# Gaps of 32 to 64 bytes between SBUF tiles, so that weight slabs and the tiles multiplied with them lie 64 bytes apart by the remainder of 128

## The chip, the core and the metric

The kernel runs on one core of one Trainium2 chip. The metric is the device time of one execution in microseconds (us). Each kernel is timed in several runs and the median is quoted; one execution of it was also recorded by the hardware profiler, and everything read from rows below is of that one execution.

## What is computed

The input is one sequence of 256 tokens with 1024 features, all in float32. It goes through two blocks.

```python
# first block, one layer
h = rms_norm(x, norm_mix)
proj = h @ w_in                       # q, k, v of three branches, gates, pool input, merge gates
a = nsa_attention(...) @ w_branch_attn
b = pool_mixer(u_pool, ...) @ w_branch_pool
x = x + (ga * a + gb * b) @ w_out
x = x + square(relu(rms_norm(x, norm_mlp) @ w_ff1)) @ w_ff2      # 4096 wide
# second block, two layers: attention in the first, a gated convolution in the second
x = x + sliding_window_attention(...)        # or short_gated_conv(...)
x = x + peer_ffn(rmsnorm(x), w_query, sub_keys, expert_u, expert_v)
# peer_ffn: for each token 8 heads pick 16 of 16384 experts by two top-16 lists of 128 keys;
# y = sum over picked e of  g_e * gelu(x . u_e) * v_e
```

The two `peer_ffn` layers are the bulk: each reads two tables (`peer_u`, `peer_v`) of 16384 x 1024 floats, and the kernel multiplies with all 16384 experts, with weights that are zero for experts that a token did not pick.

## The kernel before

**Weights as a stream.** All weight matrices are cut into slabs of 128 x 1024 floats (4096 bytes in each partition), in the order in which they are used (`plan`). The class `Stream` loads a slab into one of three buffers `wraw` (a DMA queued on SyncE), and splits it: ScalarE rounds it into `wh` (line 70), VectorE, or GpSimd for some slabs of the expert stages, writes the remainder into `wl` (line 71). `wh` and `wl` have four buffers each, and the split runs up to three slabs ahead of the slab in use, so a slab's buffers become free when TensorE is done with the slab four before it.

**Three matmuls for one.** The activations are split likewise: a tile such as `xh` holds a rounded part `xh[:, 0]` and the rest `xh[:, 1]`. Each product is three matmuls in the type fp32r: `wh` with `xh[:, 0]`, `wh` with `xh[:, 1]`, `wl` with `xh[:, 0]` (the function `dense3`). In these dense stages the weight slab is the stationary operand (128 columns, loaded into the array ahead of its matmul, rows PEld of the profile) and the activation tile is the moving operand, 256 columns (the tokens). All matmuls are issued from one helper, `mm`, line 174; the profile tells them apart by their tiles: `mm<-xh,wh` writes the PSUM tile `mm` from `xh` and `wh`.

**The stages**, in the order of the run, with the tile that is multiplied with the slabs: input projections (`xh`), the compression of keys and values (`movh`, stationary, 30 columns), pool and merge parts (`ph`, `mh`), attention output (`oh`), `w_out` and `w_ff1` (`xh`), `w_ff2` (`mid`, four tiles), the second attention (`xh`, then `xo`), and for each expert layer the query (`xh`), the 128 slabs of `peer_u` (`xh`), and the 128 slabs of `peer_v`. Between the two expert layers the convolution multiplies with `xh` and with `zh`, a tile on the place of `gA0` that the profile calls `gA`. In the `peer_v` stage (the function `mix`) the roles are turned: the activations `h` (the buffer `xh0`) are stationary, 128 columns, and the slab is the moving operand, 512 columns; the profile calls it `g<-wh,xh` and `g<-wl,xh`.

**Side work in the `peer_u` stages.** While TensorE works through the 128 slabs, VectorE does first the top-16 search (`topk`, lines 1075 to 1147), and then, in 32 groups of eight tokens, builds one-hot tables (`onehot`, lines 1175 to 1179, float16), which 16 small float16 matmuls a group turn into gate weights (`spread`; the profile calls them `g<-misc` and `g<-lows,misc`), and multiplies the results by them (line 1197). Each engine's order is the program's order here (`manual_schedule`), and the amount of side work issued with each slab is a fixed budget.

**Where tiles lie.** A pool's tiles lie one behind the other in SBUF in the order of the calls, each rounded up to 32 bytes in a partition; a tile is never moved. `x` starts at byte 4224, a multiple of 128. Behind it `cols` takes 352 bytes, and all that follows in the pool `glob` and in `xhp` has a size that is a multiple of 128, so `wraw`, `wh`, `wl`, `misc`, `row`, `xh0` and `xh1` all start at a remainder of 96 when their address is divided by 128. The built program's addresses give:

| tile | role beside the slabs `wh`, `wl` (remainder 96) | remainder before | distance before | remainder after | distance after |
|---|---|---|---|---|---|
| `xh0`, `xh1` (also `h` of `mix`) | moving; stationary in `mix` | 96 | 0 | 32 | 64 |
| `movh` | stationary, 30 columns | 32 | 64 | 32 | 64 |
| `ph`, `mh`, `oh` | moving | 0 | 32 | 32 | 64 |
| `mid` (four) | moving | 32 | 64 | 32 | 64 |
| `xo` (two) | moving | 96 | 0 | 32 | 64 |
| `zh` (place of `gA0`) | moving | 96 | 0 | 32 | 64 |

All rows and columns of these tiles that a matmul starts at lie at multiples of 128 bytes from the tile's start (but for `movh`), so the distance holds for every matmul of a row of the table. `x` stays at 0; `row`, `misc` and `wraw` stay at 96; `iota2`, `lows`, `gA1` go from 96 to 32.

Of the kernel before, what the change touches and what calls it, by code (L numbers as in the profile page):

```python
# [8 lines left out]
F32 = mybir.dt.float32  # L9
# [9 lines left out]
P = 128  # L19
# [87 lines left out]
def build(tc, a):  # L107
# [172 lines left out]
    xhp = ctx.enter_context(tc.tile_pool(name="xhp", bufs=1))  # L280

    def xh_tile(i):
        return xhp.tile([P, 2, KD, T], F32R, name=f"xh{i}")

    def sq_tile():
        return glob.tile([P, KD, T], F32, name="misc")
# [19 lines left out]
    bp = b1.enter_context(tc.tile_pool(name="b1", bufs=1))  # L306
    pa = b1.enter_context(tc.tile_pool(name="pa", bufs=1, space=PSUM))

    xh = xh_tile(0)
    sq = sq_tile()  # L310
    for i in range(0, KD, 2):
# [16 lines left out]
    kvc = bp.tile([P, 2, T], F32, name="kvc", tag="t2")  # L328
    kc2 = bp.tile([P, 2, 2, T], F32, name="kc2", tag="t4")
    mov = bp.tile([P, 2, 16, 2, 15], F32, name="mov")  # L330
    movh = bp.tile([P, 2, 2, 16, 30], F32R, name="movh")
    qr = bp.tile([P, 3, 2, T], F32, name="qr")
    qk = bp.tile([P, 3, 2, T], F32, name="qk")
# [98 lines left out]
        PE.transpose(ps[:, 0, t * 24:(t + 1) * 24], gT[:, t * P:(t + 1) * P], ident[:24, :24])  # L432
    S.activation(gates.rearrange("p t g -> p (t g)"), ps[:, 0, :48], AF.Tanh, scale=0.5)

    oh = bp.tile([P, 2, 4, T], F32R, name="oh")

    def attention():
# [268 lines left out]
    ff = ExitStack()  # L706
    fpool = ff.enter_context(tc.tile_pool(name="ff", bufs=1))
    pf = ff.enter_context(tc.tile_pool(name="pf", bufs=1, space=PSUM))
    mid = [fpool.tile([P, 2, KD, T], F32R, name=f"mid{i}") for i in range(4)]
    rel = [fpool.tile([P, 2, T], F32, name=f"rel{i}") for i in range(2)]  # L710
    sq2 = fpool.tile([P, 2, T], F32, name="sq2")
# [786 lines left out]
```

## Time and profile before

| | |
|---|---|
| median of 3 runs | 2226.88 us (2226.35 to 2228.36) |
| the profiled execution: its own time | 2228.21 us |
| its span in the trace | 2226.4 us |
| mean granted TensorE clock | 0.996 of full speed |
| TensorE busy (PE, weight loads apart) | 98% of the span |
| VectorE (DVE), ScalarE (ACT), GpSimd (POOL) busy | 72%, 49%, 7% |
| bytes moved by DMA | 382.67 MB, mean 172 GB/s |

The busy time of TensorE is that of overlapping matmuls whose ends are modelled: one matmul stands in the trace for some 280 ns, but the next starts long before that. How fast TensorE goes is therefore read from the starts of matmuls that follow each other, and this text calls the time from one start to the next the pitch.

### The profile page before, as it was taken

What the parts mean: (1) busy time and instruction counts of PE and PEld (TensorE: products, weight loads), DVE (VectorE), ACT (ScalarE), POOL (GpSimd) and SP (SyncE); (2) the same over time, 40 slices, a digit from 0 to 9 for tenths busy, and PEclk for the clock granted to TensorE, in tenths of its full rate; (3) what the DMA queues carried; (4) which work ended last, traced back from release to release, by engine and by line L of the source; (5) the groups of instructions that cost most, each with busy time, mean ns of one, the idle gap of its engine ahead of it and who ended that gap; (6) DMA issues with size and microseconds to landing.
All of it is one profiled execution on the core that took longest, in us unless ns stands there. A gap on an engine that the chain in (4) does not pass through costs nothing.

```text
span 2226.4 us, 39574 instructions
## 1 busy us (share of the span) xinstructions
PE 2186.1 (98%) x15892; PEld 2040.8 (92%) x15892; DVE 1594.8 (72%) x2802; ACT 1084.5 (49%) x1707; POOL 148.2 (7%) x66
## 2 busy tenths in 40 slices
PE   8999999999989999999999999999899999999999
PEld 7899999999989999988888889999899999888887
DVE  7757656666998899755555566779988986555555
ACT  5555555564434444445454454544444435454454
POOL 0000000001442000000000000044300000000000
PEclk9999999999999999999999999999999999999999
DMA  6435555334544444455555555545444445555554
GB/s 208 152 133 180 181 190 190 105 134 151 189 143 167 152 161 157 164 196 190 197 190 196 191 172 180 191 164 174 154 150 162 152 147 195 197 191 196 191 190 150
DMA packets 105625, 382.67 MB, mean 172 GB/s; under 512 B 11985, under 2 KB 12385, under 8 KB 105185
## 3 DMA queue, kind: packets, MB, share of 16 engines
q1 hardware_dynamic: 105120, 378.04, 48.9%
q8 instruction: 124, 2.03, 0.4%
q0 software_dynamic: 320, 2.11, 0.3%
q14 instruction: 61, 0.49, 0.1%
HBM read 379.05 MB, written 1.05 MB: 171 GB/s over the span
## 4 chain that ended last, share of the span: by engine, by line
PE 84%; DVE 10%; issue 3%; ACT 2%; DMA 1%; SPq 0%; ACTq 0%; DVEq 0%
PE mm L174 46%; PE g L174 34%; DVE wl L71 3%; PE s L174 2%; DVE gA L1117 2%; ACT wh L70 1%; PE o L174 1%; DVE gA L1115 1%; DVE gA L1114 1%; DMA wraw<-in_w_in 0%; DVE gA L1197 0%; DVE lows L1178 0%; DVE misc L1179 0%; DMA x<-in_x 0%; DVE gA L1087 0%
## 5 line engine op out<-in xcount | busy, mean ns | idle before, releaser
L71 DVE TENSOR_TENSOR wl<-wraw,wh 128x1024 fp32r<-128x1024 f32 (+1 forms) x660 | 824.0, 1249 | 512.5 <-ACT wh L70 509.1
L174 PE MATMUL mm<-xh,wh 128*128 128x256 f32 x6240 | 1148.6, 286 | 9.1 <-ACT wh L70 6.9
L70 ACT CAST wh<-wraw 128x1024 fp32r<-128x1024 f32 (+1 forms) x716 | 747.0, 1054 | 726.3 <-PE g L174 332.6
L174 PEld LDWEIGHTS mm<-xh,wh 128*128 128x128 f32 x6240 | 979.9, 193 | 11.7 <-ACT wh L70 7.5
L174 PE MATMUL mm<-xh,wl 128*128 128x256 f32 x3120 | 889.1, 285 | 13.2 <-DVE wl L71 13.2
L174 PE MATMUL g<-wh,xh 128*128 128x512 f32 x2048 | 632.6, 389 | 0.0
L174 PEld LDWEIGHTS mm<-xh,wl 128*128 128x128 f32 x3120 | 602.4, 193 | 15.5 <-DVE wl L71 15.4
L174 PEld LDWEIGHTS g<-wh,xh 128*128 128x128 f32 x2048 | 384.4, 188 | 79.8
L174 PE MATMUL g<-wl,xh 128*128 128x512 f32 x1024 | 398.4, 389 | 0.0
L174 PEld LDWEIGHTS g<-wl,xh 128*128 128x128 f32 x1024 | 192.2, 188 | 39.5
L71 POOL TENSOR_TENSOR wl<-wraw,wh 128x1024 fp32r<-128x1024 f32 x56 | 142.7, 2547 | 285.2 <-ACT wh L70 271.5
L1199 ACT ACTIVATE gA<-g 128x96 f32<-128x96 f32 (+14 forms) x72 | 23.4, 343 | 243.8 <-DVE gA L1197 225.2
L1218 DVE TENSOR_TENSOR xh<-gA,xh 128x256 fp32r<-128x256 f32 x224 | 93.5, 418 | 0.0
L1217 ACT CAST xh<-gA 128x256 fp32r<-128x256 f32 x224 | 90.1, 403 | 0.0
L174 PE MATMUL mm<-mid,wh 128*128 128x256 f32 x512 | 87.1, 276 | 0.0
L1234 ACT ACTIVATE gA<-mm 128x512 f32<-128x512 f32 (+15 forms) x112 | 55.6, 496 | 63.4 <-PE mm L174 63.4
L174 PEld LDWEIGHTS mm<-mid,wh 128*128 128x128 f32 x512 | 77.0, 188 | 0.0
L174 PE MATMUL g<-misc 128*128 128x128 f16 x512 | 67.0, 221 | 9.9 <-DVE misc L1179 9.9
L174 PEld LDWEIGHTS <-misc 128*128 128x128 f16 x1024 | 59.8, 98 | 13.1 <-issue 6.8
L174 PE MATMUL mm<-mid,wl 128*128 128x256 f32 x256 | 70.7, 276 | 0.0
L174 PE MATMUL g<-lows,misc 128*128 128x128 f16 x512 | 66.4, 220 | 0.0
L1197 DVE SCALAR_TENSOR_TENSOR gA<-g,gA 128x512 f32<-128x512 f32 (+30 forms) x114 | 57.1, 538 | 0.0
(346 smaller groups left out, 1570.2 us busy)
## 6 DMA issues: line engine op xcount, KB each, us to landing
wraw<-in_peer_u SPq DMA_DIRECT2D x256, 512.0 KB, 3.5
wraw<-in_peer_v SPq DMA_DIRECT2D x256, 512.0 KB, 3.5
wraw<-in_w_ff SPq DMA_DIRECT2D x64, 512.0 KB, 4.4
wraw<-in_w_query SPq DMA_DIRECT2D x32, 512.0 KB, 3.6
wraw<-in_w_in SPq DMA_DIRECT2D x29, 512.0 KB, 4.0
wraw<-in_w_cin SPq DMA_DIRECT2D x24, 512.0 KB, 3.6
wraw<-in_w_qkv SPq DMA_DIRECT2D x12, 512.0 KB, 4.1
wraw<-in_w SPq DMA_DIRECT2D x8, 512.0 KB, 3.5
```

The costliest lines, as they stand in the source:

```text
L70: nc.scalar.copy(h[:, s], r[:, s])
L71: (nc.gpsimd if j in self.pooled else nc.vector).tensor_sub(l[:, s], r[:, s], h[:, s].bitcast(F32))
L174: PE.matmul(out, l, r, start=start, stop=stop, skip_group_check=True)
L1114: V.tensor_tensor(eq, pb, J[:, None].to_broadcast([P, 2, NCAND, 16]), op=OP.is_equal)
L1115: V.tensor_tensor(prod, eq, code[:, hq:hq + 2, :, None].to_broadcast([P, 2, NCAND, 16]), op=OP.mult)
L1117: V.reduce_sum(sel[:, hq:hq + 2], prod.rearrange("p h c k -> p h k c"), axis=AX.X)
L1197: V.scalar_tensor_tensor(v, pr[:, i0:j], 2.0 ** -15, v, op0=OP.mult, op1=OP.mult)
L1199: S.activation(d[:, j - i0:i1 - i0, t0:t0 + 8], pr[:, j:i1], AF.Copy, scale=2.0 ** -15)
L1217: S.copy(w[0], gA(e))
L1218: V.tensor_sub(w[1], gA(e), w[0].bitcast(F32))
L1234: S.activation(d[:, :, n:], ps[:, :, n:], AF.Gelu)
```

## The change

Four small tiles that nothing reads or writes are allocated, and so push what is allocated behind them. `gap` (64 bytes) moves both `xh` and every pool opened later by 64 bytes; `gap1` moves `movh` and what stands behind it in its pool by 64 more, `gap2` moves `oh` and what follows by 32 more, `gap3` moves `mid` by 64 more. The weight slabs stay where they are. The table above has the remainders. The instructions of all engines, their order and the semaphores that they wait for are the same one by one as before; only addresses differ.

```diff
@@ -306,6 +306,8 @@
     pa = b1.enter_context(tc.tile_pool(name="pa", bufs=1, space=PSUM))
 
+
+    xhp.tile([P, 16], F32, name="gap")
     xh = xh_tile(0)
     sq = sq_tile()
@@ -328,6 +330,7 @@
     mov = bp.tile([P, 2, 16, 2, 15], F32, name="mov")
+    bp.tile([P, 16], F32, name="gap1")
     movh = bp.tile([P, 2, 2, 16, 30], F32R, name="movh")
@@ -432,6 +435,7 @@
 
+    bp.tile([P, 8], F32, name="gap2")
     oh = bp.tile([P, 2, 4, T], F32R, name="oh")
@@ -706,6 +710,7 @@
     pf = ff.enter_context(tc.tile_pool(name="pf", bufs=1, space=PSUM))
+    fpool.tile([P, 16], F32, name="gap3")
     mid = [fpool.tile([P, 2, KD, T], F32R, name=f"mid{i}") for i in range(4)]
```

## Rows read from the trace of the kernel before

**Rows 1.** The page: busy time by engine, and the chain by line

```profile
PE 2186.1 (98%) x15892; PEld 2040.8 (92%) x15892; DVE 1594.8 (72%) x2802; ACT 1084.5 (49%) x1707; POOL 148.2 (7%) x66
...
PE mm L174 46%; PE g L174 34%; DVE wl L71 3%; PE s L174 2%; DVE gA L1117 2%; ACT wh L70 1%; PE o L174 1%; DVE gA L1115 1%; DVE gA L1114 1%; DMA wraw<-in_w_in 0%; DVE gA L1197 0%; DVE lows L1178 0%; DVE misc L1179 0%; DMA x<-in_x 0%; DVE gA L1087 0%
```

**Rows 2.** Matmuls by form: count, busy us, mean ns of one, idle before

```profile
L174 PE MATMUL mm<-xh,wh 128*128 128x256 f32 x6240 | 1148.6, 286 | 9.1 <-ACT wh L70 6.9 <-ACT gA L1234 0.7 <-ACT xh L195 0.6
L174 PE MATMUL mm<-xh,wl 128*128 128x256 f32 x3120 | 889.1, 285 | 13.2 <-DVE wl L71 13.2
L174 PE MATMUL g<-wh,xh 128*128 128x512 f32 x2048 | 632.6, 389 | 0.0
...
L174 PE MATMUL mm<-mid,wh 128*128 128x256 f32 x512 | 87.1, 276 | 0.0
...
L174 PE MATMUL mm<-xo,wh 128*128 128x256 f32 x128 | 25.6, 292 | 0.6 <-ACT xo L915 0.3 <-DVE xo L916 0.2
...
L174 PE MATMUL mm<-wh,xh 128*128 128x256 f32 x64 | 12.9, 298 | 0.0
...
L174 PE MATMUL mm<-mh,wh 128*128 128x256 f32 x64 | 11.4, 279 | 0.0
```

**Rows 3.** Timeline of PE, query stage, first and last of ten groups (start, us)

```profile
504.00 0.40 PE L174 MATMUL mm<-xh,wh 128*128 128x256 f32 x2
...
507.24 0.40 PE L174 MATMUL mm<-xh,wh 128*128 128x256 f32 x2
```

**Rows 4.** Timeline of PE, `w_ff2` stage, first and last of ten groups

```profile
329.83 0.39 PE L174 MATMUL mm<-mid,wh 128*128 128x256 f32 x2
...
332.89 0.28 PE L174 MATMUL mm<-mid,wh 128*128 128x256 f32 x1
```

**Rows 5.** Timeline of PE, stage of `mh`, first and last of eleven groups

```profile
158.22 0.40 PE L174 MATMUL mm<-mh,wh 128*128 128x256 f32 x2
...
161.76 0.40 PE L174 MATMUL mm<-mh,wh 128*128 128x256 f32 x2
```

**Rows 6.** Timeline of PE, `peer_v` stage, first and last of four groups

```profile
1000.48 0.62 PE L174 MATMUL g<-wh,xh 128*128 128x512 f32 x2
...
1002.52 0.62 PE L174 MATMUL g<-wh,xh 128*128 128x512 f32 x2
```

**Rows 7.** Timeline of PE, small float16 matmuls of one group, third and last

```profile
871.59 0.22 PE L174 MATMUL g<-misc 128*128 128x128 f16 x1
...
872.33 0.22 PE L174 MATMUL g<-lows,misc 128*128 128x128 f16 x1
```

**Rows 8.** Weight loads by form: count, busy us, mean ns of one

```profile
L174 PEld LDWEIGHTS mm<-xh,wh 128*128 128x128 f32 x6240 | 979.9, 193 | 11.7 <-ACT wh L70 7.5 <-ACT xh L195 0.9 <-DVE xh L196 0.9
...
L174 PEld LDWEIGHTS g<-wh,xh 128*128 128x128 f32 x2048 | 384.4, 188 | 79.8
...
L174 PEld LDWEIGHTS mm<-mid,wh 128*128 128x128 f32 x512 | 77.0, 188 | 0.0
```

**Rows 9.** Windows in `peer_u`: length, busy PE, PEld, DVE, ACT, POOL, clock, DMA

```profile
580.00:600.00 20.00, 20.00 (x169) 20.00 (x168) 19.67 (x98) 9.28 (x11) 7.85 (x4) 1.00 0.58 193
580.00:704.00 124.00, 115.53 (x944) 114.78 (x943) 120.48 (x285) 54.15 (x63) 52.35 (x20) 0.98 0.48 165
...
1500.00:1624.00 124.00, 115.01 (x939) 114.22 (x938) 120.19 (x262) 52.09 (x61) 50.25 (x20) 0.98 0.46 160
...
860.00:880.00 20.00, 20.00 (x192) 19.87 (x191) 18.77 (x28) 8.59 (x18) 0.00 (x0) 1.00 0.46 159
892.00:917.00 25.00, 23.87 (x230) 23.54 (x226) 20.76 (x29) 8.39 (x18) 0.00 (x0) 1.00 0.41 139
```

**Rows 10.** VectorE by form: count, busy us, mean ns of one

```profile
L1175 DVE TENSOR_TENSOR misc<-iota,row 128x1024 f16<-128x1024 f16 x64 | 43.7, 683 | 0.0
...
L236 DVE TENSOR_TENSOR misc<-misc 128x512 f32<-128x512 f32 x18 | 12.4, 688 | 0.4
...
L689 DVE TENSOR_TENSOR x<-x,sq 128x512 f32<-128x512 f32 x4 | 2.8, 692 | 0.1
```

## The prediction, before the changed kernel was run

> **What bounds the kernel now.** I read the page first, then the matmuls by form, then the starts of single matmuls in each stage, then windows of the stretches where VectorE is fullest. On the page TensorE is busy 98% of the span, and the chain that ended last runs for 80% through two kinds of its matmuls, the dense ones (46%) and those of `peer_v` (34%) [rows 1]. The reader should see that waits are small: the 9360 dense matmuls on `xh` have 22.3 us of idle time before them in all [rows 2]. So in most stages the time is the number of matmuls times their pitch, and the pitch is what this change can touch.
>
> The pitch differs between stages that do the same thing. In the query stage, where slab and `xh` are 0 apart by the remainder, 27 matmuls start in 507.24 - 504.00 = 3.24 us, 120.0 ns each [rows 3]. In the `w_ff2` stage, where slab and `mid` are 64 apart, 27 start in 332.89 - 329.83 = 3.06 us, 113.3 ns each [rows 4]. With `mh`, 32 apart, 30 start in 3.54 us, 118.0 ns [rows 5]. Columns, type and slabs are the same in all three. Weight loads go along: 193 ns in the mean with `xh`, 188 with `mid` [rows 8]. So three distances are ordered as the change supposes, and its own distance, 64, has been run already, by 768 matmuls.
>
> **The change, part by part.** No instruction is added, removed or reordered, so its whole cost or gain is in the durations.
>
> *Dense matmuls at distance 0.* These are 6240 + 3120 on `xh`, 128 on `xo` with `wh` and half as many with `wl`, as many again on `zh`, and 64 + 32 with `xh` stationary [rows 2]: 9360 + 192 + 192 + 96 = 9840. Taken at `mid`'s pitch each is 120.0 - 113.3 = 6.7 ns shorter (3.24 - 3.06 us over 27): 65.6 us. Bounds: nothing, if `mid` is fast for another reason; 65.6 us, since `mid` is the fastest pitch of this size that the trace has.
>
> *Those at distance 32:* 96 on `mh`, as many on `oh` and 12 on `ph`, 4.7 ns each: 1.0 us. *`mid` and `movh`* keep their distance: 0.
>
> *The `peer_v` stage.* 2048 + 1024 matmuls of 512 columns [rows 2] go from 0 to 64 too. Their pitch is 2.04 us over 9, 226.7 ns [rows 6]. That is two times 113.3, and the float16 matmuls of 128 columns start every 0.74 us / 13 = 56.9 ns, half of it [rows 7]: 0.443 to 0.445 ns a column in all three. At distance 0 this stage thus already runs at the pace a column that the dense matmuls reach only at 64, and its weight loads take 188 ns, as with `mid`, not 193 [rows 8]. A longer moving stream seems to leave time to load weights. I take 0. Bounds: a gain of the same 6.7 ns for each weight load, 3072 x 6.7 = 20.5 us; a loss of 6.7 to 13.3 ns (once or twice, by columns, what a bad distance costs at 256), 20.5 to 41 us.
>
> *What VectorE takes back.* While TensorE gets faster, the splits and the side work stay, and where VectorE is full nothing is gained. In the window from 580 to 600 us VectorE is busy 19.67 of 20 us during 169 matmuls, so 19.67 / 169 x 24 = 2.79 us a slab [rows 9]. A slab is 24 matmuls: 2.88 us now, 2.72 after. VectorE becomes the limit from about 580 us on, and stays it until the search ends near 704 us (120.48 of 124 us busy, and TensorE already waits). The end of that stretch is then VectorE's. The gain of its 944 matmuls is lost, 6.3 us, and of the 939 in the second layer, 6.3 us [rows 9]. TensorE's waits for `wl` and the one-hot tables grow by that much.
>
> In the groups that follow, one group is 48 dense and 16 small matmuls. Late in them, from 860 to 880 us, 192 matmuls are three groups: VectorE 18.77 / 3 = 6.26 us a group, TensorE 6.67 now and 6.67 - 48 x 0.0067 = 6.35 after [rows 9]. VectorE would be 98.6% full there, just not the limit; I take off 1 us a layer, my choice between 0 and all. At the groups' end, 892 to 917 us, TensorE waits for VectorE already (23.87 of 25 us): 230 matmuls less 48 small ones lose 1.2 us, and the same in the second layer. For the start and the two attentions, where matmuls alternate with short chains on VectorE and ScalarE, I take off 2 us, without a row of their own. Together: 12.6 + 2.0 + 2.4 + 2.0 = 19.0 us. Bounds: about 10 (slack absorbs half of it), or 37 if VectorE limits all the groups, below.
>
> *Other engines.* Loads must come every 2.72 us a slab instead of 2.88; the new need is 0.524 MB / 2.72 us = 193 GB/s, which the window from 580 to 600 us already moved [rows 9]. ScalarE is about half busy. VectorE and ScalarE operands move by 64 bytes too. Of their cost a row speaks: additions of 128x512 take 688 ns with all operands at remainder 96 (line 236) and 692 with `x` at 0 and `sq` at 32 (line 689) [rows 10]. I take 0; the splits at line 71 don't move at all.
>
> *Sum.* 65.6 + 1.0 - 19.0 = 47.6 us. From the profiled execution's own 2228.2 us (span 2226.4) that gives 2180.6; the median is 1.3 us below that execution, so **2179 us**.
>
> The Trainium skill speaks against the change: "TensorE: Matmul & The Clock Gate", in the section "Step-by-step: what each phase is for", says that TensorE has two independent read ports to SBUF and that loading the next weights doesn't take bandwidth from the running matmul. By that the sum would be 0, and the time 2227 us. The pitches 120.0 and 113.3 do not agree with it, unless something else makes `mid` fast.
>
> **The rivals.**
>
> 1. *`peer_v` gains too.* The cost would hang on each weight load, whatever the moving columns: 20.5 us more, 2159 us. For it: the distance is 0 there as well. Against it: the pace a column, equal to that at distance 64, and the loads of 188 ns.
> 2. *`peer_v` loses.* 0 may be a good distance there and 64 a bad one: 20.5 to 41 us less, 2200 to 2220 us. No row has that stage at another distance, so nothing speaks for it but that.
> 3. *VectorE takes more.* If it limits all groups of each layer, their gain goes too (704 to 892 us is 28 periods of 6.7 us with 48 dense matmuls each: 28 x 48 x 6.7 ns = 9.0 us a layer): 18 us, 2197 us. For it: 98.6% leaves no room for an order of work that waits.
> 4. *The distance that counts is of 256, not 128.* `mid` now lies 64 behind the slabs by 256, `xh` will lie 192. If 192 is as good as `mh`'s 224 only (118.0 ns), the dense matmuls gain 2.0 x 9840 = 19.7 us, `mid`, which moves to 192 too, loses 4.7 x 768 = 3.6, VectorE takes 5.7 (19.0 x 2.0 / 6.7): 10 us, 2217 us.
> 5. *The change doesn't do what it says.* `mid` is fast for a reason other than its place: 2227 us. Against it: `mh` and `oh` lie between, as their distance does. By the skill's rule above this would be the outcome.
> 6. *Slower.* VectorE's one-hot comparisons (lines 1175, 1176) read `iota2` at 32 and `row` at 96 after the change, and line 1178 writes `lows` at 32 from `misc` at 96. If VectorE minds distances, these grow in a stage where it is nearly full. To turn the gain of 47.6 us into a loss over 64 groups takes 0.74 us a group beyond the free 0.09: 0.83 us over three instructions of 0.68, 0.28 us or 41% each. The 4 ns between 688 and 692 [rows 10] are far from that.
>
> **How the numbers follow.** My forecast 0.63 (its own range 2170 to 2190, by the losses of 10 to 28 us); rival 1 0.12; rival 2 0.05; rival 3 0.07; rival 4 0.05; rival 5 0.05; rival 6 0.03. A range from 2155 to 2198 holds nearly all of the first, rival 3, and most of rival 1: about 0.8. A measurement of this kernel tells 0.2% (4.5 us) from no change. Faster by more than that: all but rivals 5 and 6, 0.92; same 0.05; slower 0.03.
>
> **What would show it.** Right: starts of dense matmuls 113.3 ns apart in the query, `w_ff1`, convolution and early `peer_u` stages; their weight loads at 188 ns; `mid` unchanged; `peer_v` at 226.7 ns; VectorE still 19.9 of 20 us busy near 640 us, and TensorE's idle time before `wl` matmuls up from 13.2 us [rows 2] by about 10. Wrong: a pitch other than 113.3 ns (the distance rule fails), `peer_v` at 220 or 233 ns and more, or VectorE's instructions at other durations than before.

## The result, and the profile after

The changed kernel took 2241.5 us (median of 5 runs, 2238.36 to 2244.63), the kernel before 2228.36 us (5 runs, 2226.35 to 2231.41): ratio 1.0058, 95% interval 1.0044 to 1.0073. It is slower by 0.6% where 2.2% faster was forecast.

Every engine's work is what it was, only the pace of TensorE's matmuls differs. The page after (busy time by engine, then the chain by line) answers to [rows 1]: dense matmuls hold less of the chain (`mm`, 36% after 46%), those of `peer_v` about as much, VectorE's splits `wl` more.

```profile
PE 2192.5 (98%) x15892; PEld 2025.7 (90%) x15892; DVE 1595.2 (71%) x2802; ACT 1083.5 (48%) x1707; POOL 149.3 (7%) x66
...
PE mm L174 36%; PE g L174 33%; DVE wl L71 7%; ACT wh L70 3%; DMA wraw<-in_peer_u 2%; PE s L174 2%; DVE gA L1202 2%; DVE lows L1183 1%; PE o L174 1%; DVE gA L1122 1%; ACT act L1236 1%; ACT gA L1239 1%; DVE misc L1180 1%; DVE misc L1181 0%; DVE gA L1119 0%
```

The timeline of TensorE after (start, duration; rows between left out) shows three things. First two rows: a dense stage in its fast stretch, 9 matmuls in 189.13 - 188.11 = 1.02 us, 113.3 ns each. Next two, `w_ff1`: 27 in 3.18 us, 117.8 ns. Next two, `w_ff2` on `mid`: 27 in 3.18 us, 117.8 ns, where it was 113.3 [rows 4]. Last two, `peer_v`: 39 in 9.09 us, 233.1 ns, where it was 226.7 [rows 6].

```profile
188.11 0.39 PE L174 MATMUL mm<-xh,wh 128*128 128x256 f32 x2
...
189.13 0.39 PE L174 MATMUL mm<-xh,wh 128*128 128x256 f32 x2
...
239.83 0.40 PE L174 MATMUL mm<-xh,wh 128*128 128x256 f32 x2
...
243.01 0.40 PE L174 MATMUL mm<-xh,wh 128*128 128x256 f32 x2
...
329.93 0.40 PE L174 MATMUL mm<-mid,wh 128*128 128x256 f32 x2
...
333.11 0.40 PE L174 MATMUL mm<-mid,wh 128*128 128x256 f32 x2
...
1000.21 0.63 PE L174 MATMUL g<-wh,xh 128*128 128x512 f32 x2
...
1009.30 0.63 PE L174 MATMUL g<-wh,xh 128*128 128x512 f32 x2
```

Weight loads after, by form (count, busy us, mean ns of one, idle before), answer to [rows 8]: with `xh` they fell from 193 to 190 ns, not to 188; in `peer_v` they stand at 188 as before, though its pitch grew.

```profile
L174 PEld LDWEIGHTS mm<-xh,wh 128*128 128x128 f32 x6240 | 962.6, 190 | 17.1 <-ACT gA L1239 6.8 <-ACT wh L70 6.8 <-ACT xh L195 0.9
...
L174 PEld LDWEIGHTS g<-wh,xh 128*128 128x128 f32 x2048 | 384.8, 188 | 92.7
...
L174 PEld LDWEIGHTS mm<-mid,wh 128*128 128x128 f32 x512 | 78.2, 187 | 0.0
```

The windows after (columns as in [rows 9]) show VectorE at 19.91 of 20 us in the search, and the end of the groups, 892 to 917 us, with TensorE busy 20.31 us, where it was 23.87: it waits there for ScalarE and VectorE (rows below, with the prediction's step on VectorE). The first row is a stretch of the `qkv` stage in which TensorE was granted 0.50 of its clock, the lower level of 1.2 GHz.

```profile
389.80:396.60 6.80, 6.80 (x34) 6.80 (x33) 2.55 (x7) 1.25 (x2) 0.00 (x0) 0.50 0.46 154
580.00:600.00 20.00, 20.00 (x172) 20.00 (x171) 19.91 (x103) 9.63 (x12) 8.96 (x4) 1.00 0.62 199
...
892.00:917.00 25.00, 20.31 (x198) 19.45 (x197) 20.79 (x29) 8.40 (x18) 0.00 (x0) 1.00 0.39 127
```

The same stretch of the kernel before, in the same view, has the full clock:

```profile
389.80:396.60 6.80, 6.80 (x59) 6.80 (x60) 4.71 (x12) 1.75 (x3) 0.00 (x0) 1.00 0.46 154
```

Stage lengths, worked out as the start of a stage's first matmul to that of the next stage, say where the 13.3 us (spans 2226.4 and 2239.7) come from:

| stage | before | after | difference |
|---|---|---|---|
| `peer_v`, layers 0 and 1 | 349.49 + 354.27 | 359.64 + 364.36 | +20.2 |
| `w_ff2` (on `mid`) | 87.06 | 90.45 | +3.4 |
| `qkv` (with the half clock) | 65.00 | 67.76 | +2.8 |
| all other stages together | | | -13.1 |
| of these, `w_ff1` | 93.19 | 91.36 | -1.8 |
| of these, the searches of both `peer_u` | 166.23 + 165.74 | 163.97 + 164.47 | -3.5 |
| of these, the groups of both `peer_u` | 217.99 + 218.66 | 218.61 + 218.56 | +0.5 |

### The profile page after: what moved, and what is told of

Read it like the earlier page. It is cut to its first block, busy times and chain, and to the rows that moved or that the text cites. A ratio compares the mean times of both kernels' runs of the same rounds, so it can differ in the third digit from the quotient of the medians.

```text
span 2239.7 us, 39574 instructions
## 1 busy us (share of the span) xinstructions
PE 2192.5 (98%) x15892; PEld 2025.7 (90%) x15892; DVE 1595.2 (71%) x2802; ACT 1083.5 (48%) x1707; POOL 149.3 (7%) x66
## 4 chain that ended last, share of the span: by engine, by line
PE 73%; DVE 15%; ACT 5%; issue 3%; DMA 3%; POOL 0%; SPq 0%; ACTq 0%; DVEq 0%
PE mm L174 36%; PE g L174 33%; DVE wl L71 7%; ACT wh L70 3%; DMA wraw<-in_peer_u 2%; PE s L174 2%; DVE gA L1202 2%; DVE lows L1183 1%; PE o L174 1%; DVE gA L1122 1%; ACT act L1236 1%; ACT gA L1239 1%; DVE misc L1180 1%; DVE misc L1181 0%; DVE gA L1119 0%
## 5 line engine op out<-in xcount | busy, mean ns | idle before, releaser
L71 DVE TENSOR_TENSOR wl<-wraw,wh 128x1024 fp32r<-128x1024 f32 (+1 forms) x660 | 825.3, 1251 | 530.8 <-ACT wh L70 529.4
L174 PE MATMUL mm<-xh,wh 128*128 128x256 f32 x6240 | 1130.3, 283 | 13.6 <-ACT wh L70 6.3
L174 PEld LDWEIGHTS mm<-xh,wh 128*128 128x128 f32 x6240 | 962.6, 190 | 17.1 <-ACT gA L1239 6.8
L174 PE MATMUL mm<-xh,wl 128*128 128x256 f32 x3120 | 879.9, 282 | 14.4 <-DVE wl L71 14.4
L174 PE MATMUL g<-wh,xh 128*128 128x512 f32 x2048 | 645.7, 396 | 0.0
L174 PEld LDWEIGHTS mm<-xh,wl 128*128 128x128 f32 x3120 | 591.7, 190 | 17.3 <-DVE wl L71 17.2
L174 PE MATMUL g<-wl,xh 128*128 128x512 f32 x1024 | 404.8, 395 | 0.0
L174 PE MATMUL g<-misc 128*128 128x128 f16 x512 | 67.1, 221 | 10.9 <-DVE misc L1184 10.9
```

Of the source, the lines that this page charges most:

```text
L71: (nc.gpsimd if j in self.pooled else nc.vector).tensor_sub(l[:, s], r[:, s], h[:, s].bitcast(F32))
L174: PE.matmul(out, l, r, start=start, stop=stop, skip_group_check=True)
```

## The experiments

Three theories stood against each other. The first: the remainder of 256 counts, not of 128. The diff brought most tiles to 64 by 128, but by 256 `xh`, `mid` and `peer_v`'s tile came to 192 and only the smaller tiles (`ph`, `mh`, `oh`, `movh`) to 64. The second: places themselves count (which addresses), not distances. The third, on the part that remains: pitch isn't set by the distance alone. Beside them stood two questions of size: does `peer_v` cost the 20 us, and does VectorE take back what the dense matmuls gain? Distances below are slab minus tile by 256; the matmul means are over 764 starts of `w_ff1` (on `xh`), 768 of `w_ff2` (on `mid`) and 1531 of `peer_v` in layer 0, each in the one trace of its kernel.

**The changed kernel again**, to see what one profile repeats.

> The changed kernel, unaltered, profiled a second time. Theory A (at a distance of 64 by 128 a dense matmul can settle at one of two pitches, 113.3 or 117.7 ns, and what happened just before picks which): the same addresses, but the stretches at 113.3 ns need not be the same ones; query0, w_out and xo, each partly at 113.3 ns in the first trace, may come out otherwise, and mid may be at 113.3 again. Theory B (the distance by 256 decides: 64 fast, 192 slow): mid, xh and zh at 117.7 ns in the same places throughout. Both: peer_v at about 233 ns, time about 2241 us.

Measured: 2242.92 us (before 2231.62 beside it); 117.51, 117.78 and 233.33 ns, the means of the first profile to the hundredth. Most of the fast stretches come again too, the 113.3 ns stretch of `w_out` above among them, but not all: in the query stage of layer 1 no matmul settled at 113.3 ns in the first profile and 19% did in the second, in the search of layer 1 none and 7%. So the pitch of a stage is not fixed by the program.

**One gap of another size.** Ahead of `xh` alone, in the kernel before, with n = 8, 32, 40, 48 or 64 for 32, 128, 160, 192 or 256 bytes. Everything allocated behind it moves too:

```diff
+    xhp.tile([P, n], F32, name="gap")
     xh = xh_tile(0)
```

128 bytes:

> The kernel before with one gap of 128 bytes ahead of xh0 instead of the four gaps: xh, xo and zh stay 0 from the slabs by the remainder of 128 (128 by 256), mid stays 64 by 128 but goes from 64 to 192 by 256. Theory A: xh at 120.0 ns and peer_v at 226.7 ns as before; mid at 113.3 or 117.7 ns. Theory B: mid at 117.7 ns, xh anything but 120.0 is possible. Time: A 2227 (2230 if mid is slow), B unlike that if 128 by 256 is a place of its own.

192 bytes:

> The kernel before with one gap of 192 bytes ahead of xh0: xh, xo and zh lie 64 from the slabs by 128, and slab minus tile is 64 by 256 (192 in the changed kernel); mid goes to a distance of 0. Theory A: xh mostly at 117.7 ns with stretches of 113.3, mid at 120.0 ns, peer_v about 233 ns, time about 2243 us. Theory B: xh at 113.3 ns throughout, mid at 120.0; time near 2195 us with peer_v at 233 ns, 2175 us with peer_v at 226.7.

32 bytes:

> The kernel before with one gap of 32 bytes ahead of xh0: xh, xo and zh lie 32 before the slabs' remainder plus 128 (slab minus tile 96 by 128, as mh and oh before), mid 32 apart. Theory A: xh at about 118 ns as mh before, mid at about 118, peer_v between 226.7 and 233 ns. Theory B: xh at 118 ns too (224 by 256 as mh before). The run tells what a distance of 32 does to peer_v, on which neither has a row.

256 bytes:

> The kernel before with one gap of 256 bytes ahead of xh0: all distances by 256 are as before, those by 512 are not. If 256 is the period: xh 120.0 ns, mid 113.3 ns, peer_v 226.7 ns, 2228 us. If the period is longer (or peer_v needs the tiles at another multiple): peer_v 233.3 ns, 2248 us.

160 bytes:

> The kernel before with one gap of 160 bytes ahead of xh0: xh at slab minus tile 96 by 256, mid at 160, peer_v's operands 160 apart. Theory A for peer_v: 233.3 ns, as at each other distance but 0. For dense no forecast beyond the ones seen, between 113.3 and 120.0 ns: the run fills in two distances.

Measured, with the kernel before, the changed one and the next experiment (distance: mean pitch):

| kernel | `w_ff1` | `w_ff2` | `peer_v` | time, us |
|---|---|---|---|---|
| before | 0: 119.98 | 64: 113.36 | 0: 226.71 | 2228.36 |
| after | 192: 117.51 | 192: 117.78 | 192: 233.33 | 2241.5 |
| 128 bytes | 128: 118.66 | 192: 117.78 | 128: 233.33 | 2250.52 |
| 192 bytes | 64: 113.56 | 128: 118.67 | 64: 233.32 | 2227.94 |
| 32 bytes | 224: 116.67 | 32: 118.33 | 224: 233.33 | 2238.35 |
| 160 bytes | 96: 117.33 | 160: 119.99 | 96: 233.33 | 2246.80 |
| 256 bytes | 0: 119.97 | 64: 113.36 | 0: 226.71 | 2226.45 |
| all moved by 64 | 0: 119.99 | 64: 113.36 | 0: 226.71 | 2230.08 |

(Times of the gaps are of one run each, beside kernels before at 2226 to 2232 us.) The row that tells 128 from 256 is that of 128 bytes, which leaves `xh` at 0 by 128: by theory A `xh` stays at 120.0 and `peer_v` at 226.7 ns. They came to 118.7 and 233.3, `peer_v` with 9 matmuls in 2.10 us:

```profile
999.86 0.63 PE L174 MATMUL g<-wh,xh 128*128 128x512 f32 x2
...
1001.96 0.63 PE L174 MATMUL g<-wh,xh 128*128 128x512 f32 x2
```

The changed kernel and the one with 192 bytes both have `xh` at 64 by 128, at 192 and 64 by 256. With 192 bytes the timeline of `w_ff1` has 27 matmuls in 3.06 us, 113.3 ns; the next two rows, `peer_v` of the same kernel, have 9 in 2.10 us, 233.3 ns; the last two, late in `peer_v` of layer 1, 9 in 2.06 us, 228.9 ns:

```profile
239.93 0.39 PE L174 MATMUL mm<-xh,wh 128*128 128x256 f32 x2
...
242.99 0.39 PE L174 MATMUL mm<-xh,wh 128*128 128x256 f32 x2
...
1000.21 0.63 PE L174 MATMUL g<-wh,xh 128*128 128x512 f32 x2
...
1002.31 0.40 PE L174 MATMUL g<-wh,xh 128*128 128x512 f32 x1
...
2198.39 0.62 PE L174 MATMUL g<-wh,xh 128*128 128x512 f32 x2
...
2200.45 0.62 PE L174 MATMUL g<-wh,xh 128*128 128x512 f32 x2
```

So in these two large stages 64 by 256 gives the fast pitch for 256 columns and 192 the slow one. For 512 columns, the five distances other than 0 give 233.3 ns, but for the last 324 of 3072 matmuls at 64. That one gap of 192 bytes ends level with before (2227.94): the dense gain and `peer_v`'s loss cancel.

The small stages do not keep to this. In the changed kernel `mh` and `oh` lie at 64 by 256, yet all their matmuls ran at 117.8 ns, and with the gap of 32 bytes they lie at 192 and ran at 113.3. In the rows, `mh` in the changed kernel has 27 matmuls in 3.18 us, 117.8 ns:

```profile
154.85 0.40 PE L174 MATMUL mm<-mh,wh 128*128 128x256 f32 x2
...
158.03 0.40 PE L174 MATMUL mm<-mh,wh 128*128 128x256 f32 x2
```

In the kernel called best below `mh` lies at 64 too, and has 27 in 3.06 us, 113.3 ns:

```profile
155.73 0.39 PE L174 MATMUL mm<-mh,wh 128*128 128x256 f32 x2
...
158.79 0.39 PE L174 MATMUL mm<-mh,wh 128*128 128x256 f32 x2
```

Both distances thus have the same two pitches, 113.3 and 117.8 ns.

**Distances or places.** The gap stands ahead of everything, slabs included, so that all places move by 64 and no distance does.

```diff
+    glob.tile([P, 16], F32, name="gap")
     x = glob.tile(...)
```

> The kernel before with a gap of 64 bytes ahead of x, the first tile: every tile moves by 64 bytes and no distance changes. Theory A (distances): all pitches as before, 120.0, 113.3 and 226.7 ns, 2228 us. Rival C (a tile's own remainder counts): xh at 32 by 128 would run as in the changed kernel, 117.7 ns, and peer_v at 233.3 ns, 2241 us.

Measured: 2230.08 us, and all three pitches are those of before (last row of the table). Distances count, places don't, as far as one move by 64 bytes shows; with 256 bytes doing nothing either, the period of 256 fits.

**`peer_v` back at 0, the rest as changed.** The stationary weights `h` of `mix` get a tile of their own at distance 0:

```diff
+        hv = []
...
-            w = h[:, 0, e % 4], h[:, 1, e % 4]
+            if not hv:
+                hv.append(glob.tile([P, 2, 4, T], F32R, name="misc"))
+            w = hv[0][:, 0, e % 4], hv[0][:, 1, e % 4]
...
-            wh, wl = (h[:, p, e % 4, t * P:(t + 1) * P] for p in range(2))
+            wh, wl = (hv[0][:, p, e % 4, t * P:(t + 1) * P] for p in range(2))
...
-            res.extend((xh_tile(1), sq_tile()))
+            res.append(xh_tile(1))
...
+            res.append(sq_tile())
```

> The changed kernel, but the stationary operand of the peer_v stage lies in the buffer misc, at remainder 96 like the slabs, instead of in xh0. Theory A (the stage's pitch hangs on the distance between its two operands, 226.7 ns at 0 and 233.3 ns elsewhere): 226.7 ns, 20.2 us less than the changed kernel, about 2221 us, the dense stages as in the changed kernel. Rival C (what costs the stage 6.7 ns is not the distance, but the place of xh0 or of what the other engines write beside it): 233.3 ns, 2241 us.

Measured: 2222.58 us (10 runs), 0.9971 of before (0.9962 to 0.998). `peer_v` is back at 226.70 ns, as the timeline shows, 12 matmuls in 2.72 us; its stages at 349.47 and 354.27 us, which are before's lengths to 0.02 us.

```profile
999.88 0.62 PE L174 MATMUL g<-wh,misc 128*128 128x512 f32 x2
...
1002.60 0.62 PE L174 MATMUL g<-wh,misc 128*128 128x512 f32 x2
```

Of what the matmuls of this stage read, only the tile that TensorE holds as weights moved, and 2241.5 - 2222.6 = 18.9 us came back. This is the largest part of the loss, shown by its undoing. What is left of the change, the dense matmuls at 192, is worth 0.3%.

**The best distances together**, called best below: `xh` and `mid` at 64 by 256, `peer_v` at 0 (the edit above, with these gaps in the kernel before).

```diff
+    xhp.tile([P, 48], F32, name="gap")
     xh = xh_tile(0)
...
+    bp.tile([P, 56], F32, name="gap2")
     oh = bp.tile([P, 2, 4, T], F32R, name="oh")
...
+    fpool.tile([P, 16], F32, name="gap3")
     mid = [fpool.tile([P, 2, KD, T], F32R, name=f"mid{i}") for i in range(4)]
```

> What the runs so far favour in each stage: xh, xo, zh, ph, mh, oh and mid all at slab minus tile 64 by 256 (gaps of 192, 224 and 64 bytes), and the stationary operand of peer_v in misc, at 0. From the run with the gap of 192 (2227.9 us, peer_v 10.1 and 8.7 us longer than before, mid at 118.7 instead of 113.3 ns, 4.1 us): 2227.9 - 18.8 - 4.1 = 2205 us by theory A; by rival C 2224 us.

Measured: 2210.51 us (5 runs, 2206.82 to 2214.66), 0.9914 of before (0.99 to 0.9928), faster than both kernels. Page (busy time) and timeline (`w_ff1` at 27 matmuls in 3.06 us, 113.3 ns; `peer_v` at 12 in 2.72 us):

```profile
PE 2160.4 (98%) x15892; PEld 2013.0 (91%) x15892; DVE 1594.2 (72%) x2802; ACT 1084.8 (49%) x1707; POOL 148.5 (7%) x66
```

```profile
239.80 0.39 PE L174 MATMUL mm<-xh,wh 128*128 128x256 f32 x2
...
242.86 0.39 PE L174 MATMUL mm<-xh,wh 128*128 128x256 f32 x2
...
999.94 0.62 PE L174 MATMUL g<-wh,misc 128*128 128x512 f32 x2
...
1002.66 0.62 PE L174 MATMUL g<-wh,misc 128*128 128x512 f32 x2
```

It is 19.1 us faster than the kernel before beside it (2229.57 us, 15 runs), 5.5 us short of the 2205 expected here and far from the 47.6 us of the prediction. Not all stages run at 113.3 ns even at distance 64. Of the matmuls of `w_ff1`, 94% stand in stretches at 113.3 ns (means of nine starts), of `w_ff2` all, of the first convolution matmuls (`xh`) 93%, of the second (`zh`) all; of the query stage of layer 0 none, of layer 1 8%, of the search of layer 0 35%, of its groups 2%. The slow ones stand at 117.8 ns. One distance thus has two pitches.

**Is the pitch drawn anew?** An added matmul of 8, 16, 24, ... columns stands ahead of each slab of `w_ff2` (its result isn't read), to disturb TensorE's rhythm by a different amount each time; once on the changed kernel (`mid` at 192), once on the best one (`mid` at 64).

```diff
+                    if kick is not None:
+                        u = (i + j) * (kt // KD) + q
+                        mm(kick[:, 0, :8 * u + 8], w[0][:, :P], xh[0][:, 0, 0, :8 * u + 8], True, True)
```

At 192:

> The changed kernel with one more matmul, whose result nobody reads, ahead of each of the 32 slabs of w_ff2: 8 columns ahead of the first, 16 ahead of the second, and so on to 256. mid lies at slab minus tile 192 by 256 there. Theory A (two settled pitches, and what has just run picks one): within the stage some slabs run at 113.3 ns a matmul and others at 117.8, changing only at the added matmuls. Rival D (the pitch of a stretch comes from its addresses, or from what other engines do at the time): 117.8 ns throughout, as in three of three traces without the additions. Cost of the added matmuls themselves: about 32 x 0.12 = 3.8 us at most.

Measured: 2243.59 us; all 32 slabs settle at 117.78 ns.

At 64:

> The same additions in the fastest version so far, where mid lies at 64 by 256 and ran at 113.3 ns throughout. Theory A: some slabs fall to 117.8 ns, fewer than at 192 are slow. Rival D: 113.3 ns throughout.

Measured: 2214.53 us; of 32 slabs, 13 settle at 113.33 ns (slabs 0, 4, 7, 10, 13, 15, 17, 20, 22, 23, 24, 25 and 28) and the others at 117.78; the pitch switches only at an added matmul. The timeline shows two neighbours, the added matmul (`s<-mid,wh`) between them. Ahead of it 18 matmuls in 364.48 - 362.44 = 2.04 us, 113.3 ns; behind it 18 in 367.40 - 365.28 = 2.12 us, 117.8 ns, with the same tiles, the same distance and the full clock:

```profile
362.44 0.39 PE L174 MATMUL mm<-mid,wh 128*128 128x256 f32 x2
...
364.48 0.39 PE L174 MATMUL mm<-mid,wh 128*128 128x256 f32 x2
364.82 0.26 PE L174 MATMUL s<-mid,wh 128*128 128x216 f32 x1
364.91 0.41 PE L174 MATMUL mm<-mid,wh 128*128 128x256 f32 x2
365.28 0.40 PE L174 MATMUL mm<-mid,wh 128*128 128x256 f32 x2
...
367.40 0.40 PE L174 MATMUL mm<-mid,wh 128*128 128x256 f32 x2
```

So at distance 64 two settled pitches exist, and how the run of matmuls begins decides between them; once begun, a run keeps its pitch. This agrees with the third theory. What in the beginning picks it, the runs don't show.

This run says one thing more. Up to `w_ff2` it has the order and the addresses of best, and yet its `w_ff1` settles at 113.3 ns for 6% of the matmuls, where best had 94%; the rows have 27 matmuls in 242.87 - 239.69 = 3.18 us, 117.8 ns:

```profile
239.69 0.40 PE L174 MATMUL mm<-xh,wh 128*128 128x256 f32 x2
...
242.87 0.40 PE L174 MATMUL mm<-xh,wh 128*128 128x256 f32 x2
```

So one trace of a stage is one draw. What the distance does show over all traces is the share of draws: of the matmuls on `xh`, `xo` and `zh`, 30 to 59% settled at 113.3 ns in the four kernels with these tiles at 64, 6 to 10% in the four traces with them at 192, none in the three kernels with them at 0 (all near 120.0). `mid` at 64 was fast throughout in five of five traces without added matmuls, and at 192 slow in four of four.

**VectorE's load in the groups, less by one instruction:** on the best kernel, one of the two float16 products of a group goes to GpSimd.

```diff
-                V.tensor_mul(lo[b], hi[b], tok(glT, t0))
+                G.tensor_mul(lo[b], hi[b], tok(glT, t0))
```

> The fastest version so far with one of VectorE's four one-hot instructions of each group (the low part, 0.69 us) done by GpSimd. Theory E (the dense gain in the 32 groups is lost because VectorE sets the end of that stage): VectorE's load falls by about a tenth, the group stages fall from 217.9 to about 214 us each, 2203 us. If VectorE is not the limit there, or GpSimd slows VectorE by as much: 2210 us or more.

Measured: 2250.55 us (4 runs), 1.0099 of before (1.0082 to 1.0116); the groups stages grew from 217.9 to 238.8 us in layer 0. Two rows by form say why: the product takes 2110 ns on GpSimd, where the same line takes 686 on VectorE, and VectorE's next step waits 46.2 us for it.

```profile
L1181 POOL TENSOR_TENSOR lows<-misc,row 128x1024 f16<-128x1024 f16 x64 | 135.1, 2110 | 339.2 <-DVE misc L1179 167.1 <-PE g L174 104.5 <-DVE gA L1239 67.7
...
L1182 DVE TENSOR_TENSOR misc<-misc,row 128x1024 f16<-128x1024 f16 x64 | 48.0, 750 | 46.2 <-POOL lows L1181 46.2
```

The splits at line 71 went from 1252 ns in the best kernel to 1316 ns as well. VectorE was not relieved but made to wait, so the run says nothing on whether it sets the groups' end.

## Why the prediction was wrong, by its own steps

**The step that failed is "The `peer_v` stage ... I take 0".** Its 3072 matmuls went from 226.7 to 233.3 ns: 3072 x 6.63 ns = 20.4 us, and the stages grew by 20.2. This turned the sign. The reasoning there, that equal pace a column means that the distance costs nothing with 512 columns, read a good distance as no dependence on the distance. The bounds that were kept beside it held this: it is the lower end of rival 2, one more 6.7 ns for each matmul, at a chance of 0.05. The kernel with `peer_v` back at 0 shows it, and all five other distances cost as much over layer 0.

**"Taken at `mid`'s pitch each is 6.7 ns shorter"** failed too. In settled stages it was 120.0 - 117.8 = 2.2 ns, 9840 x 2.2 = 22 us in place of 65.6. There are two causes. The remainder of 128 puts 64 and 192 together, which differ in how often a run of matmuls takes the fast pitch (rival 4, whose 2.0 ns for the dense matmuls was close, though it took 192 for one slow pitch). And `mid`'s 113.3 ns is one of two pitches at its distance, so even at 64 by 256 it isn't the pitch of every stage: the best kernel still has whole stages at 117.8, and `mh` and `oh`, brought to 64 by this change, stayed at 117.8.

**"`mid` and `movh` keep their distance: 0"** holds by 128 only. `mid` moved by 128 and lost 3.4 us, near the 3.6 us of rival 4.

Rivals 2 and 4 were priced as alternatives, yet both came true at once. Rival 4's gain of 10 us and rival 2's loss of 20.5 us together give 2227 - 10 + 20.5 = 2237 us; with the 2.8 us of `qkv`, 2240, against 2241.5 measured. That this comes so near is in part luck: the 2.8 us belong to neither rival, and what VectorE takes was only estimated in rival 4.

**The clock.** The half clock between 389.8 and 396.6 us made `qkv` 2.8 us longer and had no step in the prediction. Ahead of it, from 382 to 389 us, TensorE was busy 5.87 of 7 us, waiting for the norm's short chain, as it did before the change (6.09 of 7). A stretch of this kind, between 380 and 401 us, is in ten of the fourteen profiles, not in those of before, the gaps of 192 and 256 bytes and the last experiment. The kernel with all places moved by 64 has it too, though all its distances and pitches are those of before, so it comes without the change as well; the changed distances are not needed for it:

```profile
392.90:396.30 3.40, 3.40 (x17) 3.40 (x18) 0.94 (x6) 0.03 (x1) 0.00 (x0) 0.50 0.87 282
```

**"What VectorE takes back"** was right in place, not settled in size. In the searches, from the matmul that started at 580 us before (1500 us in layer 1) to the first one-hot matmul, 1844 matmuls gained 2.2 ns each, 4.1 us, and the stretches grew shorter by 0.8 and 0.4 us, so most was lost; but in the two kernels with the pitches of before (256 bytes, all moved by 64) the same stretches come out up to 2.3 us shorter, so the size stays open. In the groups hardly anything came through, where the prediction took off 1 us a layer and the end: from the first to the last group's first one-hot matmul there were 704.5 to 917.39 us before, 212.89, and 702.92 to 915.80 after, 212.88; in the best kernel 212.93. In 23 of the 26 group stages of the thirteen profiles other than the last experiment's, it is 212.8 to 213.0 us, at dense pitches from 116.6 (32 bytes) to 120.0 ns (128 bytes), and in the other three 215. So TensorE's pitch does not set this length. In the changed kernel the periods (start to start of a group's first one-hot matmul) fell from 6.73 to 6.65 us, and the last three took back what 28 had gained (7.48, 8.03 and 7.11 us in place of 6.73, 6.73 and 5.53). The waits by what ended them (us in all, times, longest) say for whom TensorE waits more. For `wl` it is 14.4 us after 13.2 [rows 2], for the one-hot tables (`misc`, line 1184) 10.9 after 9.9, so neither grew by the 10 us or so that the prediction named as its sign. New are six waits of 5.7 us for ScalarE's reading of the results (`gA`, line 1239), one of 0.7 before [rows 2]. The first row is of before, three are of after, and the last is ScalarE's own wait at the end of the groups, from 890 to 916 us: it waits there for VectorE's multiplication (line 1202).

```profile
PE g L174 <- DVE misc L1179: 9.9, 4, 3.4
...
PE mm L174 <- DVE wl L71: 14.4, 11, 3.0
PE g L174 <- DVE misc L1184: 10.9, 4, 3.8
...
PE mm L174 <- ACT gA L1239: 5.7, 6, 1.2
...
ACT gA L1204 <- DVE gA L1202: 15.7, 3, 5.2
```

This agrees with rival 3, that VectorE limits the groups. That TensorE's pitch doesn't is shown by the lengths above; that VectorE does is argued, since the experiment meant to relieve it failed.

**Rival 6 is refuted.** VectorE's forms after (count, busy us, mean ns) are those of [rows 10]: the comparisons at 683 and 686 ns, splits at 1252 (1251 before).

```profile
L1180 DVE TENSOR_TENSOR misc<-iota,row 128x1024 f16<-128x1024 f16 x64 | 43.7, 683 | 0.0
...
L1181 DVE TENSOR_TENSOR misc<-iota,row 128x1024 f16<-128x1024 f16 x64 | 43.9, 686 | 0.0
```

**Rival 5** is refuted for both sizes of matmul: both pitches changed. The Trainium skill's rule behind it ("TensorE: Matmul & The Clock Gate", section "Step-by-step: what each phase is for": two independent read ports, so that loading weights doesn't slow the running matmul) does not agree with these runs: the place of the stationary tile alone moved `peer_v` from 233.3 to 226.7 ns. The measurement decides; by what way the place acts, no run shows.

## What to carry to other kernels

Read a matmul's pitch from starts, by stage, and set it beside the distance between its two operands by 256 bytes; try a distance on each matmul shape apart, since 64 gave the fast pitch most often here for 256 columns and 0 always for 512. A stage that is already at the best pace a column is evidence that its present place is good, not that its place is free: move it only on purpose. And before a gain in pitch is counted, ask whether one fast stage is the rule of its distance or one draw (profile the same kernel again), and which engine ends the stage once TensorE is faster.

## What was unexpected of the hardware

- The pitch of fp32r matmuls depends on the distance between operands in SBUF, with a period of 256 that the gaps of 128 and 256 bytes fit: for 256 columns, in `w_ff1` or `w_ff2` of the traces above, 120.0 ns at 0, 118.3 at 32, 113.3 at 64, 117.3 at 96, 118.7 at 128, 120.0 at 160, 117.8 at 192, 116.7 at 224; for 512 columns 226.7 at 0 and 233.3 at 64, 96, 128, 192 and 224. Other stages at the same distance can differ: `mh` at 224 ran at 117.8 [rows 5], the groups at 128 at 120.0. Why 0 is the best for the one size and among the worst for the other is open.
- At distances 64 and 192, matmuls of 256 columns settle at 113.3 or 117.8 ns, by how their run began, and keep it until it is disturbed; 64 takes the fast pitch more often. At 64, matmuls of 512 columns once settled at 228.9 instead of 233.3.
- A float16 product of 128x1024 took 2110 ns on GpSimd and 686 on VectorE, and VectorE's splits went from 1252 to 1316 ns meanwhile.
